# Strassen's seven products in an up projection, and a down projection with tokens on partitions

## The chip, the cores and the metric

One core of one Trainium2 chip. The metric is the device time of one execution in microseconds; the kernel before has a median of 2528.21 us over three runs (2526.31 to 2530.2).

## What is computed

One layer of a hybrid decoder trunk on 1040 tokens (16 learned meta tokens and 1024 others) of width 1024, in float32. Only the last part is touched in earnest:

```python
mixed = jax.nn.sigmoid(g_attn) * y_attn + jax.nn.sigmoid(g_ssd) * y_ssd      # y_ssd = y @ w_o_ssd, y: 2048 wide
h = layer_norm(DEEPNORM_ALPHA * h + mixed @ w_out[i], ln1_g[i], ln1_b[i])
u = causal_dwconv(h @ w_up, conv_w, conv_b)                                  # 1024 -> 2 x 2816, width 3 in time
gate, val = jnp.split(u, 2, axis=-1)
ffn = (jax.nn.silu(gate) * val) @ w_down                                     # 2816 -> 1024
h = layer_norm(DEEPNORM_ALPHA * h + ffn, ln2_g[i], ln2_b[i])
return h[:, N_META:]
```

`h` is the embedding after its own LayerNorm. Ahead of this come the input projections, latent attention in eight heads and a state-space mixer (SSD) in four groups; they stay as they are.

## The kernel before

Features lie on partitions (blocks of 128) and tokens on the free axis, in three chunks of about 348 tokens with a few tokens of overlap for the convolutions. A product is done at float32 accuracy by three passes: each operand is split into a rounded high half (ACT, L152 and L174) and the remainder (DVE, L153 and L175), and `mm3` (L158, matmuls at L163 to L165) adds high x high, low x high and high x low in PSUM. `load_w` (L138) fetches a weight block through two `wraw` buffers on the SP queue and splits it at a raised priority.

The instructions stand in the program in the order of the code; the scheduler of the framework orders each engine's queue by priority (place in the program, `load_w` ahead of its place by 400 in this part) and by when its model thinks operands and buffers are there. A tile of a pool opened over the memory of a closed one waits for the tiles that lay there. PSUM has eight banks, shared out by `cut_psum` (L109).

In the part touched:

- `transposed` (L297) stores h to HBM by chunk, and the section that starts at L635 (attention output, attention gate) reads it back and splits it. The tail of the SSD section computes gates (`gs_gate`, L745) from these tiles; four of the eight gates come after the last SSD group.
- Mixer outputs and LN1 (L899 to L981), a chunk at a time: `load_y` (L906) loads 16 tiles of y and 4 of factors and splits them; 8 output blocks with w_o_ssd (16 x 3 matmuls each), merged with the gates; 8 with w_out (8 x 3 matmuls), h added; `ln1_begin` (L921) takes the mean by a product with ones (L924), subtracts it, sums squares; `inv_root` (L177) sums over partitions (L184), takes the root on 128-partition columns (L198) and broadcasts it (L193). Weights are loaded anew in each chunk.
- FFN (L983 to L1101): `FF_PARTS` (L85) cuts the 22 blocks of the hidden width into five parts of four and one of two. `up` (L995) makes one block of the up projection for a chunk (24 matmuls), the convolution (ACT L1002, DVE L1005 twice) and Silu (L1008); `glu` (L1011) multiplies and splits. After each part the down projection adds its share to 24 SBUF accumulators (L1044 to L1047). `FHEAD` (L89) sets the first block's work on chunks 0 and 1 ahead of chunk 2, whose LN1 is still running. The last two blocks go with tokens on partitions (`last_down`, L1053, matmuls L1073 to L1075), with the accumulators added by products with ident (L1077), and LN2 follows on rows (L1081 to L1095).

## Time and profile before

| | |
|---|---|
| median of three runs | 2528.21 us |
| profiled execution | 2525.36 us |
| its span, first to last instruction | 2523.6 us |
| mean granted clock | 0.995 |
| busy: PE, DVE, ACT, GpSimd (POOL) | 2466.9, 1627.5, 1064.8, 8.5 us |
| matmuls recorded | 16023 |

PE is TensorE's matmul engine, PEld its weight loads, DVE the vector engine, ACT the scalar engine, SP the queue that issues nearly all DMAs. A busy share is the union of an engine's records; a matmul's record is longer than its share of the stream, since matmuls are pipelined, so prices are read from start times of matmuls that follow each other. PEclk is the granted clock as a share of 2.4 GHz.

### The profile page before, as it was taken

The numbers are of one execution on the slowest core, as the hardware profiler recorded it, in microseconds if no ns is written. First come the engines' busy times: TensorE is split into PE (matmuls) and PEld (weight loads), VectorE is DVE, ScalarE is ACT, GpSimd is POOL, SyncE is SP. The second block draws the span as 40 slices with busy tenths as digits, with TensorE's granted clock in tenths as the row PEclk, the third lists the DMA queues.
The fourth block names the chain that finished last, engine by engine and source line by source line (L and its number), as shares of the span: only waits on it lengthen the run. The fifth ranks groups of instructions, "written<-read, shape, count | busy, mean of one in ns | idle before, by whom it ended". The sixth has DMA issues, their size and how long they took to land.

```text
span 2523.6 us, 41608 instructions
## 1 busy us (share of the span) xinstructions
PE 2466.9 (98%) x16023; PEld 2376.7 (94%) x16023; DVE 1627.5 (64%) x4071; ACT 1064.8 (42%) x2420; POOL 8.5 (0%) x62
## 2 busy tenths in 40 slices
PE   6999999999999999999999999999999999999997
PEld 6999899899999999999999999999999999999997
DVE  6467677683356877777777568777565454554567
ACT  6345455562245554555454335444313131323331
POOL 0000000000000000000000000000000000000000
PEclk9999999999999999999999999999999999999999
DMA  5121011142222212122221566754111111111122
GB/s 201 46 65 44 27 38 44 38 138 78 67 103 91 84 62 95 66 79 82 68 89 53 168 203 209 223 167 147 36 58 39 55 42 51 47 47 51 43 86 82
DMA packets 96221, 215.22 MB, mean 85 GB/s; under 512 B 11542, under 2 KB 57366, under 8 KB 93974
## 3 DMA queue, kind: packets, MB, share of 16 engines
q1 hardware_dynamic: 95734, 211.51, 26.1%
q8 instruction: 126, 2.06, 0.3%
q0 software_dynamic: 288, 1.05, 0.1%
q14 instruction: 73, 0.60, 0.1%
HBM read 179.06 MB, written 31.35 MB: 83 GB/s over the span
## 4 chain that ended last, share of the span: by engine, by line
PE 86%; DVE 6%; DMA 4%; issue 1%; ACT 1%; SPq 0%; DVEq 0%; ACTq 0%
PE g L165 23%; PE g L163 23%; PE g L164 23%; PE c L577 3%; DMA yl<-y_d 2%; PE c L830 2%; PE c L854 1%; PE c L571 1%; PE c L834 1%; DMA wraw<-wos 1%; DVE wl L153 1%; PE c L524 1%; PE c L526 1%; PE c L528 1%; PE c L527 1%
## 5 line engine op out<-in xcount | busy, mean ns | idle before, releaser
L163 PE MATMUL g<-h,wh 128*128 128x348 f32 (+5 forms) x2616 | 845.3, 323 | 5.7 <-ACT lat L359 4.7
L165 PE MATMUL g<-h,wh 128*128 128x348 f32 (+5 forms) x2616 | 846.3, 324 | 1.2 <-DVE h L978 1.0
L164 PE MATMUL g<-h,wl 128*128 128x348 f32 (+5 forms) x2616 | 844.8, 323 | 0.0
L152 ACT CAST wh<-wraw 128x512 fp32r<-128x512 f32 (+2 forms) x474 | 287.3, 611 | 561.5 <-PE g L165 473.2
L163 PEld LDWEIGHTS g<-h,wh 128*128 128x128 f32 x2616 | 492.9, 188 | 9.6 <-ACT lat L359 5.0
L165 PEld LDWEIGHTS g<-h,wh 128*128 128x128 f32 x2616 | 492.6, 188 | 5.3 <-DVE h L978 2.9
L164 PEld LDWEIGHTS g<-h,wl 128*128 128x128 f32 x2616 | 493.4, 189 | 2.5 <-issue 2.3
L153 DVE TENSOR_TENSOR wl<-wraw,wh 128x512 fp32r<-128x512 f32 (+2 forms) x474 | 320.5, 678 | 234.8 <-ACT wh L152 229.0
L163 PE MATMUL g<-a,wh 128*128 128x348 f32 (+3 forms) x936 | 301.7, 322 | 1.6 <-DVE kn L175 1.1
L165 PE MATMUL g<-a,wh 128*128 128x348 f32 (+3 forms) x936 | 300.3, 321 | 0.0
L164 PE MATMUL g<-a,wl 128*128 128x348 f32 (+3 forms) x936 | 299.9, 320 | 0.0
L1005 DVE SCALAR_TENSOR_TENSOR u<-g,V,u 128x332 f32<-128x332 f32 (+2 forms) x264 | 150.8, 572 | 127.1 <-ACT u L1002 123.1
L163 PEld LDWEIGHTS g<-a,wh 128*128 128x128 f32 x936 | 176.2, 188 | 2.3 <-DVE kn L175 1.4
L165 PEld LDWEIGHTS g<-a,wh 128*128 128x128 f32 x936 | 176.0, 188 | 0.6 <-DVE a L175 0.5
L164 PEld LDWEIGHTS g<-a,wl 128*128 128x128 f32 x936 | 176.2, 188 | 0.0
L735 DVE SCALAR_TENSOR_TENSOR xc<-g,V,xc 128x347 f32<-128x347 f32 (+2 forms) x180 | 103.7, 576 | 41.6 <-ACT xc L731 38.8
L163 PE MATMUL g<-yh,wh 128*128 128x334 f32 (+2 forms) x384 | 122.8, 320 | 1.8 <-ACT wh L152 1.8
L165 PE MATMUL g<-yh,wh 128*128 128x334 f32 (+2 forms) x384 | 123.3, 321 | 0.0
L164 PE MATMUL g<-yh,wl 128*128 128x334 f32 (+2 forms) x384 | 122.6, 319 | 0.3 <-DVE wl L153 0.3
L1002 ACT ACTIVATE u<-g,V 128x332 f32<-128x332 f32 (+2 forms) x132 | 83.5, 633 | 78.3 <-PE g L165 76.6
L1047 DVE TENSOR_TENSOR a<-a,g 128x332 f32<-128x332 f32 (+2 forms) x96 | 49.0, 510 | 96.0 <-PE g L165 96.0
L820 ACT ACTIVATE G<-ac,tok 116x116 f32<-116x116 f32 x288 | 91.6, 379 | 42.4 <-PE c L830 42.4
(241 smaller groups left out, 3631.5 us busy)
## 6 DMA issues: line engine op xcount, KB each, us to landing
wraw<-win SPq DMA_DIRECT2D x65, 512.0 KB, 3.3
wraw<-wup SPq DMA_DIRECT2D x54, 512.0 KB, 3.3
wraw<-wos SPq DMA_DIRECT2D x48, 512.0 KB, 4.3
ac<-cs_d SPq DMA_DIRECT2D x16, 1044.0 KB, 5.7
wraw<-wout SPq DMA_DIRECT2D x24, 512.0 KB, 3.4
wraw<-wdn SPq DMA_DIRECT2D x40, 256.0 KB, 2.7
xt<-x SPq DMA_DIRECT2D x9, 512.0 KB, 5.2
wraw<-wqb SPq DMA_DIRECT2D x12, 384.0 KB, 3.7
```

The lines of the kernel that those rows point to most:

```text
L152: nc.scalar.copy(h[:, :n * ncol], r)
L153: nc.vector.tensor_sub(l[:, :n * ncol], r, f32(h[:, :n * ncol]))
L163: nc.tensor.matmul(ps, ah, bh, start=(k == 0), stop=False)
L164: nc.tensor.matmul(ps, al, bh, start=False, stop=False)
L165: nc.tensor.matmul(ps, ah, bl, start=False, stop=(k == n - 1))
L577: nc.tensor.matmul(ops[:, o0:n], vt[j][:w, hh * P:(hh + 1) * P], ptt[:w, o0:n], start=(j == 0), stop=(j == nbmax - 1))
L735: nc.vector.scalar_tensor_tensor(t[:, l:n], ps[:, hal + l - s:hal + n - s], vec("cw", (3 - s) * 24 + ct), t[:, l:n], ALU.mult, ALU.add)
L820: nc.scalar.activation(G_[:, k * S:(k + 1) * S], ac[:S, hh, C0[b] + k * S:C0[b] + (k + 1) * S], AF.Relu, bias=tok[:, 3 * b + k, 32 + hd:33 ...
L830: nc.tensor.matmul(yd[64 * hh:64 * hh + 64, k * S:(k + 1) * S], xd[:, k, hh], G[hh][:, k * S:(k + 1) * S], start=True, stop=True)
L1002: nc.scalar.activation(t[:, :n], ps[:, 2:n + 2], AF.Identity, bias=vec("fb", ti), scale=vec("fw", 2 * 44 + ti))
L1005: nc.vector.scalar_tensor_tensor(t[:, :n], ps[:, 2 - s:n + 2 - s], vec("fw", (2 - s) * 44 + ti), t[:, :n], ALU.mult, ALU.add)
L1047: nc.vector.tensor_add(A[:, :n], A[:, :n], ps[:, :n])
```

## The change

- Mixer outputs and LN1 go by two halves of 514 tokens (two of overlap) in place of three chunks; a product over 514 tokens is two matmuls of 258 and 256 columns into a pair of PSUM banks (`mm3h`).
- LN1 needs no mean: w_out is centred over its output features as it is loaded (GpSimd subtracts `wm`, the row means of w_out, for which all of w_out is loaded again as `wor` and summed), and h is centred where it is read back (`h_centered`), and kept in HBM as `hc_d`.
- Up projection by Strassen's scheme in its form with seven products: the weights of block f and f + 22 (gate and value) are cut in halves of the input width, and the tokens into two halves. Of the eight products of quarter blocks seven are left, on sums of weight quarters (GpSimd, then split) and on sums of token halves (`T1` to `T4`, formed once after LN1). The products of the first token half need LN1 of that half alone; for three blocks (`NHEAD`) these are put ahead.
- The gated products go to HBM (`gv_d`). The down projection then has tokens on partitions throughout: stationary operand 128 tokens of a hidden block, moving operand 512 columns of w_down, all 22 blocks summed in PSUM, two rounds of four token tiles; the residual enters PSUM as transposes of h1 (read back from HBM). LN2 on rows as before.
- Pools and PSUM pairs are laid out anew, some from the right end of SBUF.

The diff's core:

```diff
+HB = (NEED, NEED + 512)
+HN = 514
+HC = ((0, 258), (258, 514))
+NHEAD = 3
+KBLK = ((0, 4), (4, 8), (8, 12), (12, 17), (17, 22))
...
+            if center is not None:
+                r3 = raw[:, :kt * ncol].rearrange("p (k n) -> p k n", n=ncol)
+                nc.gpsimd.tensor_tensor(r3, r3, center.broadcast_to([P, kt, ncol]), ALU.subtract)
...
+    def mm3h(ps, lhs, rhs, start=True):
...
+            for i, (a, b) in enumerate(((ah, bh), (al, bh), (ah, bl))):
+                for c0, c1 in HC:
+                    nc.tensor.matmul(ps[:, PO + c0:PO + c1], a, b[:, c0:c1], start=(start and k == 0 and i == 0),
...
+        for c in range(3):
+            h_back(c)
+            h_centered(c)
...
+    cut_psum(0, 3)
+    pf1 = eF.enter_context(pool("F1", 16))
+    p = eD.enter_context(pool("Dr", 1, "right"))
+    pm = eM.enter_context(pool("Dm", 17, "right"))
+    pyh = eW.enter_context(pool("Dy", 33, "right"))
...
+    for k in range(KT):
+        raw = wp.tile([P, KT * P], F32, name="wraw", tag="wraw", bufs=2)
+        nc.sync.dma_start(raw, wor[k])
+        nc.vector.reduce_sum(wm[:, k], raw, axis=AX.X)
...
+    for hi in range(2):
...
+            W = load_w(wout[m], KT, center=wm)
...
+        if hi == 1:
+            eM.close()
+            pf2 = eF.enter_context(pool("F2", 40))
+            pz = eD.enter_context(pool("Dz", 8, "right"))
+        rd = inv_root(ssq, HN, 1.0 / D, LN_EPS)
...
+            for j in range(hB):
+                b11, b21 = ftile(pz, F32), ftile(pz, F32)
+                nc.sync.dma_start(b11, h1_d[j][:, HB[0]:HB[0] + HN])
+                nc.sync.dma_start(b21, h1_d[j + hB][:, HB[0]:HB[0] + HN])
+                b12, b22 = normed(j), normed(j + hB)
+                nc.vector.tensor_sub(b11, b12, b11)
+                x = dtmp("t2", "yl" if j < 3 else "ml", 3)
+                nc.vector.tensor_sub(x, b22, b11)
+                T2[j] = form(pf2, x)
+                nc.gpsimd.tensor_sub(b21, b21, x)
...
+    cut_psum(0, 4)
+    eD.close()
+    pe = eF.enter_context(pool("E1", 1))
+    rhs = {1: B1[:hB], 2: B1[hB:], 3: B2, 4: T4, 5: T1, 6: T2, 7: T3}
...
+            nc.gpsimd.tensor_sub(s3, a11, a21)
+            w[7] = wsplit(pe, s3, 5)
+            nc.gpsimd.tensor_add(s1, a21, a22)
+            nc.gpsimd.tensor_sub(s2, s1, a11)
+            w[6] = wsplit(pe, s2, 5)
+            w[5] = wsplit(pe, s1, 5)
+            nc.gpsimd.tensor_sub(s2, a12, s2)
+            w[3] = wsplit(pe, s2, 5)
+            w[4] = wsplit(pe, a22, 5)
...
+            x0 = q["x0"]
+            prod(x2, 7, w)
+            prod(x0, 6, w, False)
+            u2, u4 = etile("u2", 2), etile("u4", 2)
+            nc.scalar.copy(u2, half(x0))
+            x1 = dpair()
+            prod(x1, 2, w)
+            c11 = q["p1"]
+            nc.vector.tensor_add(c11, c11, half(x1))
+            ga = conv_up(c11, f, "ga", NHEAD)
+            prod(x0, 5, w, False)
+            nc.scalar.copy(u4, half(x0))
+        nc.vector.tensor_add(u4, u4, half(x2))
+        vb = conv_up(u4, f + NFF, "va", 2)
+        if f + 1 < NFF:
+            first(f + 1)
+        prod(x0, 3, w, False)
...
+        prod(x2, 4, w, False)
+        nc.vector.tensor_mul(gb, gb, vb)
+        nc.sync.dma_start(gv_d[f][:, 512:], gb)
+        nc.vector.tensor_add(u2, u2, half(x2))
+        va = conv_up(u2, f + NFF, "va", 2)
+        nc.vector.tensor_mul(ga, ga, va)
+        nc.sync.dma_start(gv_d[f][:, :512], ga)
...
+        for r in range(2):
+            hr = load_r(r)
...
+                        for j in range(KT):
+                            nc.tensor.matmul(pss[j // 4][:, (j % 4) * P:(j % 4) * P + P], hr[j][:, o], ident,
+                                             start=(j % 4 == 0), stop=False, is_transpose=True)
...
+                                nc.tensor.matmul(pss[q], a, b, start=False, stop=(k == NFF - 1 and i == 2))
```

## Rows read from the trace of the kernel before

**Rows 1.** The page: busy time by engine, and PE in 40 slices.
```profile
PE 2466.9 (98%) x16023; PEld 2376.7 (94%) x16023; DVE 1627.5 (64%) x4071; ACT 1064.8 (42%) x2420; POOL 8.5 (0%) x62
...
PE   6999999999999999999999999999999999999997
```
**Rows 2.** Stretches: length, busy time of each engine, PEclk, DMA share, GB/s.
```profile
545.00:740.00 195.00, 194.52 (x1244) 193.51 (x1243) 85.81 (x165) 65.79 (x147) 0.41 (x4) 1.00 0.30 97
1437.00:1660.00 223.00, 212.38 (x1315) 208.27 (x1314) 167.80 (x338) 101.84 (x192) 0.00 (x0) 0.98 0.65 204
1660.00:1765.00 105.00, 102.89 (x635) 99.51 (x634) 76.22 (x151) 49.74 (x88) 1.19 (x2) 1.00 0.50 165
1765.00:2422.00 657.00, 657.00 (x4177) 657.00 (x4176) 336.86 (x605) 192.90 (x346) 0.00 (x0) 1.00 0.15 47
2422.00:2513.20 91.20, 86.23 (x619) 83.83 (x617) 72.02 (x184) 25.08 (x50) 0.00 (x0) 0.98 0.25 84
2513.20:2523.60 10.40, 0.05 (x1) 0.00 (x0) 7.04 (x24) 0.00 (x0) 0.00 (x0) 0.71 0.38 135
```
**Rows 3.** Timeline of PE: start, duration; first and last of two unbroken runs.
```profile
172.57 0.28 PE L163 MATMUL g<-wh,a 128*116 128x256 f32 x1
...
178.83 0.28 PE L165 MATMUL g<-wl,a 128*112 128x256 f32 x1
...
2459.15 0.32 PE L163 MATMUL g<-h,wh 128*128 128x350 f32 x1
...
2461.88 0.32 PE L165 MATMUL g<-h,wh 128*128 128x350 f32 x1
```
**Rows 4.** Line 1077: count and durations of the additions by ident.
```profile
L1077 PE MATMUL c<-K,a x144: 270/274/422, 2441.3 to 2513.0; 128*128 128x128 f32 x96, 128*76 128x128 f32 x16, 128*92 128x128 f32 x16, 128*88 128x128 f32 x16
```
**Rows 5.** Timeline of PE after the last gap but one.
```profile
2499.37 0.82 PE L1073 MATMUL c<-h,a 128*88 128x256 f32 x5 [3.35 <-ACT a L174]
...
2501.38 0.41 PE L1075 MATMUL c<-h,a 128*88 128x256 f32 x1
...
2502.02 0.41 PE L1075 MATMUL c<-h,a 128*88 128x256 f32 x1
```
**Rows 6.** The chain that ended last: start, length, what.
```profile
195.86 0.89 PE c L571 x9
...
1433.51 6.00 DMA yl<-y_d
...
1536.90 0.80 PE c L924 x2
...
1740.86 0.80 PE c L184 x6
1746.45 1.46 DVE r L975 x3
```
**Rows 7.** The stretch of the last gates, columns as in rows 2.
```profile
1404.00:1440.00 36.00, 36.00 (x233) 36.00 (x232) 16.35 (x32) 11.35 (x26) 0.00 (x0) 1.00 0.66 198
```
**Rows 8.** Waits of PE: us in total, times, longest.
```profile
PE g L163 <- ACT mx L954: 4.2, 2, 2.9
...
PE g L163 <- ACT wh L152: 1.8, 1, 1.8
```
**Rows 9.** DVE and ACT by line and form: busy us, mean ns, idle before.
```profile
L153 DVE TENSOR_TENSOR wl<-wraw,wh 128x512 fp32r<-128x512 f32 x296 | 203.5, 690 | 126.2 <-ACT wh L152 122.8
...
L1093 DVE SCALAR_TENSOR_TENSOR yt<-c,mv,g 128x512 f32<-128x512 f32 x8 | 5.8, 747 | 3.7 <-DMA out<-yt 3.7
...
L152 ACT CAST wh<-wraw 128x512 fp32r<-128x512 f32 x296 | 181.7, 620 | 433.8 <-PE g L165 355.5 <-DMA wraw<-wos 41.9 <-issue 14.6
L1002 ACT ACTIVATE u<-g,V 128x348 f32<-128x348 f32 x44 | 28.2, 640 | 47.4 <-PE g L165 47.4
```
**Rows 10.** GpSimd by line and form.
```profile
L741 POOL MEMSET xc<- 128x4 f32 x20 | 2.0, 101 | 776.8 <-DVE y L867 453.4 <-PE c L780 170.8 <-DVE ga L655 152.6
L553 POOL MEMSET p<- 111x112 f32 x8 | 1.6, 195 | 0.0
```
**Rows 11.** DMA issues: count, KB each, median us to landing.
```profile
wraw<-wup SPq DMA_DIRECT2D x54, 512.0 KB, 3.3
```

More of the change, by code (lines that the diff above doesn't have):

```diff
@@ L88 @@
 WPRIO = (35, 400)
-FHEAD = 1
 LATB = 7
@@ L100, in tile_hybrid @@
 def tile_hybrid(ctx: ExitStack, tc: tile.TileContext, x, vecs, consts, cos, sin, win, wqb, wk, wv,
-                woa, wos, wout, wup, wdn, wdl, ln2, out):
+                woa, wos, wout, wor, wup, wdl, ln2, out):
     nc = tc.nc
@@ L171, in ctile, with dpair, half @@
         return psum["c"].tile([P, 512], F32, name="c", tag="c")
+    def dpair():
+        return psum["d"].tile([P, 1024], F32, name="d", tag="d")
+    def mm3h(ps, lhs, rhs, start=True):
+        n = len(lhs)
+        for k in range(n):
+            (ah, al), (bh, bl) = lhs[k], rhs[k]
+            for i, (a, b) in enumerate(((ah, bh), (al, bh), (ah, bl))):
+                for c0, c1 in HC:
+                    nc.tensor.matmul(ps[:, PO + c0:PO + c1], a, b[:, c0:c1], start=(start and k == 0 and i == 0),
+                                     stop=(k == n - 1 and i == 2), skip_group_check=not start)
+    def half(ps):
+        return ps[:, PO:PO + HN]
     def split(H, L, src):
@@ L180, in inv_root @@
         ps = ctile()
-        starts = [min(j * P, n - P) for j in range(-(-n // P))]
+        groups = [(0, n)] if n <= 512 else HC
+        starts = [a + min(j * P, b - a - P) for a, b in groups for j in range(-(-(b - a) // P))]
         k = len(starts)
@@ L195, in inv_root @@
             done = e
-        return res[:, :n]
+        return res
     def rsqrt_cols(r, v, t):
@@ L702, in tile_hybrid, with h_centered @@
                 h[k][c] = (H, L)
+                hfs[k] = of
+        def h_centered(c):
+            n = C1[c] - lo(c)
+            off = lo(c) - E0[c]
+            sm_ = p3.tile([P, 352], F32, name="hs", tag="hf", bufs=9)
+            for k in range(1, KT):
+                nc.vector.tensor_add(sm_[:, :n], (hfs[0] if k == 1 else sm_)[:, off if k == 1 else 0:][:, :n],
+                                     hfs[k][:, off:off + n])
+            ps = ctile()
+            nc.tensor.matmul(ps[:, :n], ones, sm_[:, :n], start=True, stop=True)
+            nc.scalar.activation(sm_[:, :n], ps[:, :n], AF.Copy, scale=1.0 / D)
+            for k in range(KT):
+                nc.vector.tensor_sub(hfs[k][:, off:off + n], hfs[k][:, off:off + n], sm_[:, :n])
+                nc.sync.dma_start(hc_d[k][:, lo(c):C1[c]], hfs[k][:, off:off + n])
+        for c in range(3):
+            h_back(c)
+            h_centered(c)
         for m in range(3):
@@ new lines, in prod, with etile, conv_up @@
+    def prod(ps, q, w, start=True):
+        mm3h(ps, w[q], rhs[q], start)
+    def etile(name, bufs, n=HN):
+        return pe.tile([P, n], F32, name=name, tag=name, bufs=bufs)
+    def conv_up(src, ti, tag, bufs):
+        t = etile(tag, bufs, 512)
+        nc.scalar.activation(t, src[:, 2:], AF.Identity, bias=vec("fb", ti), scale=vec("fw", 2 * 44 + ti))
+        for k in (1, 2):
+            nc.vector.scalar_tensor_tensor(t, src[:, 2 - k:HN - k], vec("fw", (2 - k) * 44 + ti), t, ALU.mult, ALU.add)
+        if ti < NFF:
+            nc.scalar.activation(t, t, AF.Silu)
+        return t
@@ new lines, in tile_hybrid, with first @@
+    st = [dict() for _ in range(NFF)]
+    def first(f):
+        q = st[f]
+        if f < NHEAD:
+            q["w"] = wrest(f, None)
+            return
+        q["w"] = wrest(f, {})
+        q["x0"] = dpair()
+        prod(q["x0"], 1, q["w"])
+        q["p1"] = etile("p1", NHEAD)
+        nc.scalar.copy(q["p1"], half(q["x0"]))
+    tops = {}
+    for f in range(NHEAD):
+        tops[f] = wtop(f)
+        q = st[f]
+        q["x0"] = dpair()
+        prod(q["x0"], 1, tops[f])
+        q["p1"] = etile("p1", NHEAD)
+        nc.scalar.copy(q["p1"], half(q["x0"]))
+        for g in ([f - 1] if f else []) + ([f] if f == NHEAD - 1 else []):
+            x = st[g].pop("x0")
+            prod(x, 2, tops[g], False)
+            st[g]["ga"] = conv_up(half(x), g, "ga", NHEAD)
@@ new lines, in load_g, with load_r @@
+        def load_g(r, k):
+            with tc.high_priority(wprio[0]):
+                t = p.tile([P, 512], F32, name="gv", tag="gv", bufs=3)
+                nc.sync.dma_start(t, gv_d[k][:, 512 * r:512 * r + 512])
+                H = ph.tile([P, 512], F32R, name="dh", tag="dh")
+                L = ph.tile([P, 512], F32R, name="dl", tag="dl")
+                split(H, L, t)
+            return H, L
+        def load_r(r):
+            res = []
+            with tc.high_priority(wprio[0]):
+                for k in range(KT):
+                    t = p.tile([P, 512], F32, name="hr", tag="hr", bufs=8)
+                    nc.sync.dma_start(t, h1_d[k][:, OUT0 + 512 * r:OUT0 + 512 * r + 512])
+                    nc.scalar.activation(t, t, AF.Copy, scale=ALPHA)
+                    res.append(t)
+            return res
@@ L1141, in _prepare @@
     wup = full(inp["w_up"][0], 2 * NFF, KT)
-    wdn = full(inp["w_down"][0], KT, NFF)
-    wdl = np.stack([inp["w_down"][0][f * P:(f + 1) * P] for f in range(*FF_PARTS[-1])])
+    wor = inp["w_out"][0].reshape(KT, P, D)
+    wdl = inp["w_down"][0].reshape(NFF, P, D)
     vecs = np.zeros((P, NVC), np.float32)
```

412 lines of the change are left out of this document (207 added, 205 removed).

## The prediction

> **What bounds the kernel now.** I read the page first: TensorE (PE) is busy 2466.9 us of a span of 2523.6, and no slice of the span but the first and the last is below nine tenths [rows 1]. So the columns streamed through PE set the time. The profiled execution took 2525.4 us; the median of the three runs, 2528.2, is 0.11% more, and I add that at the end. 0.2% (5 us) is about what a measurement of this kernel can tell from no change.
>
> Then the stretches from the first mixer output (1437 us) on, which hold all that is edited but a small piece [rows 2]. PE is idle there for 10.6 us (to 1660), 2.1 (to 1765), 0 (657 us of up and down projection without a gap), 5.0, and for the last 10.4 us, in which only the last LayerNorm and the store run: 28 us. Where the clock column is below 1, matmuls ran partly at 1.2 GHz: 0.02 x 223 + 0.02 x 91 = 6 us more. So 34 us of this part are not column time.
>
> Then the start times of matmuls in a row [rows 3], since durations overlap. 256 columns: 172.57 to 178.83 us over 53 steps, 118.1 ns. 350 columns: 2459.15 to 2461.88 over 17 steps, 160.6 ns. That is 0.461 and 0.459 ns a column: no fixed price of a matmul can be seen, and each has a weight load of its own. So halving a matmul is free down to 256 columns. 512 columns don't occur; in proportion they take 235 ns, by the line through 256 and 350 columns 232.
>
> **The sum, PE.** Up projection before: 44 blocks x 8 x 3 matmuls at 334, 346 and 350 columns, 1056 x 1030 x 0.46 ns = 500 us. After: 22 blocks x 7 products x 4 x 3 matmuls over 514 columns, each cut into 258 and 256 (237 ns): 1848 x 0.237 = 438 us. **-62.** Matmuls rise from 3168 to 3696, columns fall by an eighth.
>
> Down projection before: 20 blocks x 8 x 3 over 1024 columns, 480 x 1024 x 0.46 = 226 us; the last two blocks 216 x 0.118 = 25.5; their additions of the residual by ident, 144 records [rows 4] at the 0.099 us of a transpose (nine in 0.89 us [rows 6]), 14. After: 1056 x 0.235 = 248, and 64 transposes of h1, 6. **-11.**
>
> Mixer outputs before 576 x 1034 x 0.46 = 274 us, after 1152 x 0.237 = 273. The three ones products for the mean (0.8 us each [rows 6]) go, and the column sums and broadcasts of inv_root drop from 18 to 10 each: **-4** together. PE in all: **-77.**
>
> **The sum, waits.** The 34 us above all belong to seams that are rebuilt, so I take them out and price the new seams.
>
> (a) Start of the mixer outputs. Before, the y tiles of a third come in while the last gates run, at 198 GB/s [rows 7], with DMA waits for y in the chain of up to 6 us [rows 6]. Now the y of half of the tokens must be there for the first output, 20 tiles of 263 KB, and wm needs all of wor (8 x 524 KB) ahead of them in program order, on the same SP queue and the same two wraw buffers: 3.4 MB become 9.5 MB, 30 us more at that rate. That overlaps with output m = 0 (11.4 us) and with what slack the gates leave. I take 14; bounds 2 (the wait there before, 1.8 [rows 8]) and 28. For the second half the y tiles load under w_out (46 us): 3.
>
> (b) The last output of a half goes through DVE, DVE, ACT, DVE before w_out can use it; before, these waits were 4.2 us, two of them [rows 8]. 3; bounds 0 and 6.
>
> (c) LN1 of the second half up to the first Strassen product that needs it. After the last w_out product: residual, square, sum (2.4 us); column sums to normalised rows (1740.86 to 1746.45, 5.6 us [rows 6]); then on DVE 8 normalisations, 8 differences and 20 low halves, 36 x 0.69 to 0.75 us [rows 9] = 26 us. That makes 34 us, of which T2 and T3 (products 6 and 7) are ready after some 25. PE has the six head products of B1, 6 x 2.85 = 17 us. The weights of products 7 to 4 lie in E1, opened where Dz and Dr were; I assume that some wait for the last form (no row shows placement). 17; bounds 8 and 25. In the kernel before FHEAD covered this seam to 2.1 us with two whole chunks of tokens.
>
> (d) Within the up projection PE takes 7 x 2.85 = 19.9 us a block. DVE: 7 low halves x 0.69, 8 convolution steps and 3 sums x 0.75, 2 products x 0.69 = 14.5 us; ACT 7 x 0.62 + 9 x 0.7 = 10.6 [rows 9]. Covered in the mean; a PSUM pair must be read between two products into it, which another product (2.85 us) covers except in the first three blocks. 5; bounds 0 and 25. The products' stores and loads add 0.5 MB a block to a queue that moves 47 GB/s in this stretch [rows 2]: nothing.
>
> GpSimd takes the weight sums, four of 512 columns a block, and 1024 columns for each w_out block. No row has such an operation; the nearest is a fill of 112 columns in 195 ns against 101 ns for four columns [rows 10], so 0.5 us at least for 512, and at most perhaps three times DVE's 0.69, 2 us. I take 1.1, nearer to the fill, beside other work.
>
> (e) Up to down. hr lands where p1, ga and the last operands lay: conversion of the last block (some 6 us), a DMA (3.3 us for 512 KB [rows 11]), the scale, then the transposes that open the accumulation. 12; bounds 6 and 18.
>
> (f) The end: last LayerNorm and store, 10.4 us before [rows 2]; the piece is of the same size: 9, bounds 8 and 11.
>
> (g) The clock. After the gap of 3.35 us PE ran 256 columns in 213 ns instead of 118 (2501.38 to 2502.02, three steps [rows 5]), which is the 1.2 GHz level, for some 3 us: 1.7 us for each of the three long gaps, 5.
>
> (h) Centring h when it is read back: 45 DVE operations of about 0.52 us in a stretch where DVE is busy 86 of 195 us [rows 2], three PE products of 0.8, 24 stores: 1; bounds 0 and 6.
>
> New seams: 14 + 3 + 3 + 17 + 5 + 12 + 9 + 5 + 1 = 69. Sum: 2525.4 - 77 - 34 + 69 = 2483, and with 0.11% **2486 us**.
>
> **Two rules weighed.** The matmul price carries everything: 0.46 ns a column at 256 and at 350 columns [rows 3]. The Trainium skill (TensorE: Matmul & The Clock Gate, Back-to-back issue gap) gives a stream of load and matmul about 81 ns at 128 and 131 ns at 512 columns, mostly a fixed price; an estimate between these is 98 ns at 257 and 109 at 343, by which the up projection would go from 345 to 362 us, a loss where I count a gain of 62. The rows of this trace contradict it.
>
> DVE's 690 ns for a difference of 512 columns [rows 9] were measured with GpSimd idle, which was busy 8.5 us in all [rows 1]. The Trainium skill (SBUF - State Buffer, Who interferes with whom) says that a DVE instruction with two SBUF inputs and a GpSimd one that reads SBUF exclude each other for a whole instruction. No run here shows that yet.
>
> **The rivals.**
> 1. The seams stay as cheap as before: wor loaded under the gates, weights of E1 not held. For it: only 2.1 us at the LN1 seam before. Against it: the bytes of (a) and DVE's 26 us of (c). 2525.4 - 77 = 2448, with 0.11% 2451.
> 2. Late DVE: if its 14.5 us and GpSimd's 4 x 1.1 can't overlap, they make 18.9 of 19.9 us, and queues in order then hold a PSUM pair now and then, 1.5 us a block: +33, 2519.
> 3. **Slower: GpSimd sets the pace.** If DVE has to wait out each sum of t us, a block takes 14.5 + 4t once that passes 19.9. The change loses when a block is 2.2 us longer than PE needs, t = 1.9; at t = 2.5 it is 22 x 4.6 = 101 us, 2587. For it: no row bounds t firmly. Against it: 2 us is three times DVE's own.
> 4. Pairs of halves cost more than the runs of 256 columns do. Up projection and mixer outputs have 6000 of them, so the change loses from 126 ns a piece instead of 118.5; at 130 ns +69, 2555. For it: no row has pairs on one weight tile in two PSUM banks. Against it: 53 even steps [rows 3].
> That seven products were not seven eighths of the columns is excluded by the code: 22 x 7 x 12 x 514 against 44 x 24 x 1030.
>
> **Chances.** Forecast 0.57, rival 1 0.20, rival 2 0.15, rival 3 0.05, rival 4 0.03. Within the forecast (a), (c), (d) and (e) may each be off by about 10, together some 20: 2466 to 2506. The range takes in rival 1 and most of rival 2: 2446 to 2518. Faster by over 0.2% means below 2523: the first three cases but for a tail of rival 2, 0.90; within 0.2% 0.03; slower 0.07.
>
> **What would show it.** Right: in the up stretch starts 0.118 us apart, 19.9 us a block, PE full; 512-column matmuls 0.235 us apart; gaps at the start of the mixer outputs (released by DMA of y), at LN1 (by forms of T2, T3 or by wl) and at the first transposes (by hr), with a granted clock below 1 after each. Wrong: starts further apart than 0.12 us at full clock (rival 4); PE waiting on ACT or DVE in every block with DVE over 90% busy, its 512-column differences well above 0.69 us (rivals 2 and 3); no gap over 5 us at the seams (rival 1).

## The result, and the profile after

The changed kernel takes **2679.49 us** (median of four runs, 2674.55 to 2684.01) against 2529.2 for the kernel before beside it: a ratio of **1.0595** [1.0573, 1.0617]. The forecast was 2486 with a range up to 2518, so it is missed by 193 us and on the wrong side.

The page answers to [rows 1]: PE's busy time is the same (2463.5 us against 2466.9) in a span of 2672.8, so it is idle for 209 us instead of 57. The slices below nine tenths begin where the mixer outputs begin, and those of the clock stand with them; the mean granted clock is 0.956 (0.995 before).

```profile
PE 2463.5 (92%) x16451; PEld 2322.7 (87%) x16451; DVE 1646.7 (62%) x3819; ACT 1111.7 (42%) x2434; POOL 174.8 (7%) x174
...
PE   6999999999999999999996897978888878879998
...
PEclk9999999999999999999998997988989888889999
```

By stretches (columns as in [rows 2]): h read back and attention output; mixer outputs and w_out of the first half, then of the second; LN1 to the first products that need it; the up projection; the seam to the down projection; the first part of that.

```profile
545.00:740.00 195.00, 189.00 (x1178) 186.09 (x1177) 98.91 (x198) 57.45 (x126) 0.29 (x3) 0.98 0.36 117
...
1440.00:1620.00 180.00, 150.77 (x1208) 149.42 (x1206) 93.90 (x128) 52.19 (x86) 15.50 (x8) 0.92 0.51 167
1620.00:1760.00 140.00, 124.06 (x961) 121.91 (x962) 84.36 (x130) 49.91 (x84) 11.39 (x6) 0.90 0.50 163
1760.00:1830.00 70.00, 47.91 (x353) 47.17 (x352) 49.48 (x74) 29.94 (x51) 22.92 (x14) 0.80 0.36 121
1830.00:2380.00 550.00, 466.11 (x3482) 460.98 (x3481) 306.21 (x426) 200.41 (x328) 116.52 (x85) 0.89 0.20 62
2380.00:2420.00 40.00, 23.76 (x144) 20.36 (x143) 20.81 (x31) 20.86 (x35) 1.23 (x2) 0.79 0.66 229
2420.00:2540.00 120.00, 120.00 (x532) 97.48 (x531) 63.84 (x120) 47.72 (x85) 0.00 (x0) 1.00 0.56 189
```

No long stretch is full but the down projection. In 550 us of up projection PE is idle for 84 and the clock is 0.89; before, [rows 2] had 657 us without a gap at a clock of 1.00. No other engine is the bound there: DVE is busy 56%, ACT 36%, GpSimd 21%. So PE waits for something that is late, not for something that is full. PE's waits name it (us in total, times, longest):

```profile
PE d L191 <- ACT u L1191: 75.5, 19, 5.0
PE d L191 <- ACT wh L160: 26.9, 1, 26.9
...
PE c L1285 <- ACT hr L1251: 15.4, 3, 7.9
PE d L191 <- ACT r L1028: 14.4, 1, 14.4
PE d L191 <- ACT f L198: 13.1, 5, 10.2
```

Nineteen times, once in each block that has no products put ahead, a product waits for the copy `u4` (L1191), which empties a PSUM pair between two products into it. PE's order there is Strassen's products 3 and 4 of one block, 7, 6, 2 and 5 of the next, and 1 of the block after that; `u4` takes product 5 out of the pair before product 3 of the same block goes into it, and product 1 is its cover. The other four rows are the seams: the start of the mixer outputs, the transposes of the down projection, LN1 to up projection, and the second half's y.

**One block in the timeline** shows why the copy is late. L1086 loads weights into one of two landing buffers, L1109 to L1115 are the sums on GpSimd, L198 and L199 a cast and a low half, L1191 is the copy; rows of PE are L191.

```profile
2016.21 0.80 PE L191 MATMUL d<-f,wh 128*128 128x258 f32 x2 [3.98 <-ACT u L1191]
...
2024.93 0.62 ACT L198 CAST wh<-wraw 128x512 fp32r<-128x512 f32 x1 [1.81 <-issue]
...
2025.59 0.69 DVE L199 TENSOR_TENSOR wl<-wraw,wh 128x512 fp32r<-128x512 f32 x1
...
2026.31 0.33 SPq L1086 DMA_DIRECT2D wraw<-wup  x1
...
2030.17 1.28 POOL L1109 TENSOR_TENSOR s<-wraw 128x512 f32<-128x512 f32 x1 [20.13 <-DMA wraw<-wup]
...
2031.40 1.30 POOL L1111 TENSOR_TENSOR s<-wraw 128x512 f32<-128x512 f32 x1
...
2032.14 1.11 DVE L199 TENSOR_TENSOR wl<-s,wh 128x512 fp32r<-128x512 f32 x1 [3.04 <-ACT wh L198]
2032.78 1.62 POOL L1112 TENSOR_TENSOR s<-s,wraw 128x512 f32<-128x512 f32 x1
...
2035.86 1.30 POOL L1115 TENSOR_TENSOR s<-wraw,s 128x512 f32<-128x512 f32 x1 [1.46 <-DVE wl L199]
...
2037.18 15.08 SPq L1086 DMA_DIRECT2D wraw<-wup  x2
...
2040.48 0.62 ACT L198 CAST wh<-wraw 128x512 fp32r<-128x512 f32 x1 [3.25 <-DMA wraw<-wup]
...
2042.58 0.56 ACT L1191 COPY u<-d 128x514 f32<-128x514 f32 x1
...
2043.19 0.80 PE L191 MATMUL d<-f,wh 128*128 128x258 f32 x2 [3.88 <-ACT u L1191]
```

Read it backwards from 2043.19. The copy ran at 2042.58. It stood in ACT's queue behind a cast of fresh weights (2040.48), for which ACT had been idle for 3.25 us, and behind two more casts and a Silu; the fresh weights are for a later block, and nothing on PE was waiting for them. They came late because their load could be issued only at 2037.18, when GpSimd's last sum (L1115) had read the buffer's old content. That sum came after the three sums ahead of it, and the first of these waited for the other landing buffer (load issued at 2026.31). That buffer was freed by the low half at 2025.59, whose cast (2024.93) takes a weight tile that Strassen's product 4 gives up; the profile names no releaser for this cast, but by the code the tile is that one, and PE finished product 4 at about 2024.9. So there is a **loop through the two landing buffers**: from the end of product 4 to the restart of PE it takes 2043.2 - 2024.9 = 18.3 us. PE has five products to do in that time, 5 x 2.89 = 14.4 us; the difference, 3.9 us, is the gap. After the gap that ends at 2016.21 PE runs at the 1.2 GHz level for some 6 us (six matmuls in 1.29 us from 2016.80, in 0.72 from 2022.76), 2.9 us lost. Together 20.2 + 3.9 + 2.9 = 27.0 us a block, 2016.21 to 2043.19, where 19.9 was forecast.

The clock's part differs from block to block: after the gaps PE worked for 2.8 to 5.9 us at the lower level. This is the stretch of 17 blocks, from one restart of PE to another (columns as in [rows 2]):

```profile
1909.32:2367.25 457.93, 384.96 (x2857) 381.05 (x2857) 242.35 (x340) 163.87 (x271) 92.69 (x68) 0.88 0.19 59
```

A block takes 26.9 us on average: PE is idle for 4.3 of them, and its 2857 matmuls, 344 us at the full-clock spacing of 0.1204, took 385.0, so that 2.4 us a block are lost at the lower level.

### The profile page after: what moved, and what is told of

It is laid out like the page before. It is cut to its first block, busy times and chain, and to the rows that moved or that the text cites. A ratio compares the mean times of both kernels' runs of the same rounds, so it can differ in the third digit from the quotient of the medians.

```text
span 2672.8 us, 42479 instructions
## 1 busy us (share of the span) xinstructions
PE 2463.5 (92%) x16451; PEld 2322.7 (87%) x16451; DVE 1646.7 (62%) x3819; ACT 1111.7 (42%) x2434; POOL 174.8 (7%) x174
## 4 chain that ended last, share of the span: by engine, by line
PE 74%; DMA 8%; DVE 6%; POOL 3%; issue 3%; ACT 3%; SPq 0%; DVEq 0%; POOLq 0%; ACTq 0%
PE d L191 15%; PE g L171 11%; PE g L173 11%; PE g L172 11%; PE c L1294 9%; DMA wraw<-wup 5%; PE c L605 3%; PE c L881 2%; ACT wh L198 2%; PE c L905 1%; PE c L599 1%; POOL s L1112 1%; DVE wl L199 1%; PE c L885 1%; POOL s L1111 1%
## 5 line engine op out<-in xcount | busy, mean ns | idle before, releaser
L191 PE MATMUL d<-f,wh 128*128 128x258 f32 (+1 forms) x4000 | 693.4, 296 | 142.6 <-ACT u L1191 75.5
L191 PEld LDWEIGHTS d<-f,wh 128*128 128x128 f32 x4000 | 591.6, 203 | 151.2 <-ACT u L1191 79.5
L171 PE MATMUL g<-h,wh 128*128 128x348 f32 (+3 forms) x1560 | 507.2, 325 | 8.8 <-ACT h L198 4.8
L172 PE MATMUL g<-h,wl 128*128 128x348 f32 (+3 forms) x1560 | 507.5, 325 | 0.0
L173 PE MATMUL g<-h,wh 128*128 128x348 f32 (+3 forms) x1560 | 507.0, 325 | 0.0
L191 PE MATMUL d<-f,wl 128*128 128x258 f32 (+1 forms) x2000 | 423.0, 294 | 0.0
L191 PEld LDWEIGHTS d<-f,wl 128*128 128x128 f32 x2000 | 331.1, 202 | 0.4 <-DVE wl L161 0.2
L171 PEld LDWEIGHTS g<-h,wh 128*128 128x128 f32 x1560 | 294.9, 189 | 12.4 <-ACT h L198 5.2
L172 PEld LDWEIGHTS g<-h,wl 128*128 128x128 f32 x1560 | 295.0, 189 | 2.4 <-issue 2.4
L173 PEld LDWEIGHTS g<-h,wh 128*128 128x128 f32 x1560 | 294.5, 189 | 2.8 <-issue 2.4
L199 DVE TENSOR_TENSOR wl<-wraw,wh 128x512 fp32r<-128x512 f32 x154 | 102.3, 689 | 161.3 <-ACT wh L198 127.6
L198 ACT CAST wh<-wraw 128x512 fp32r<-128x512 f32 x154 | 90.8, 617 | 239.7 <-PE c L1294 100.3
L199 DVE TENSOR_TENSOR wl<-s,wh 128x512 fp32r<-128x512 f32 x88 | 72.8, 828 | 157.5 <-ACT wh L198 157.2
L171 PE MATMUL g<-a,wh 128*128 128x348 f32 (+2 forms) x456 | 148.8, 326 | 1.5 <-DVE kn L199 1.1
L173 PE MATMUL g<-a,wh 128*128 128x348 f32 (+2 forms) x456 | 148.2, 325 | 0.0
L172 PE MATMUL g<-a,wl 128*128 128x348 f32 (+2 forms) x456 | 147.7, 324 | 0.0
L198 ACT CAST wh<-s 128x512 fp32r<-128x512 f32 x88 | 54.1, 619 | 214.6 <-POOL s L1109 101.2
```

The source lines that it names most:

```text
L171: nc.tensor.matmul(ps, ah, bh, start=(k == 0), stop=False)
L172: nc.tensor.matmul(ps, al, bh, start=False, stop=False)
L173: nc.tensor.matmul(ps, ah, bl, start=False, stop=(k == n - 1))
L191: nc.tensor.matmul(ps[:, PO + c0:PO + c1], a, b[:, c0:c1], start=(start and k == 0 and i == 0), stop=(k == n - 1 and i == 2), skip_group_c ...
L198: nc.scalar.copy(H, src)
L199: nc.vector.tensor_sub(L, src, f32(H))
```

## The experiments

Medians, ratios to the kernel before run beside each, and what each came to against the changed kernel (2679.5). The last column compares different sessions, in which the kernel before took between 2528.3 and 2531.8 us, so that differences of some 3 us in it mean nothing:

| run | edit | us | ratio, 95% | |
|---|---|---|---|---|
| e1 | third landing buffer | 2590.4 | 1.0239 [1.0215, 1.0264] | -89 |
| e2 | copy ahead of the casts | 2584.2 | 1.0217 [1.0194, 1.0240] | -95 |
| e6 | weight sums on DVE | 2569.6 | 1.0164 [1.0140, 1.0187] | -110 |
| e3 | eight plain products | 2597.0 | 1.0271 [1.0246, 1.0295] | -83 |
| e7 | LN1's PSUM pair, down seam | 2671.9 | 1.0569 [1.0552, 1.0586] | -8 |
| e8 | start of both mixer halves | 2652.6 | 1.0484 [1.0467, 1.0500] | -27 |
| e9 | e2, e6, e7, e8 together | 2520.0 | 0.9967 [0.9954, 0.9980] | -160 |
| e10 | e3 with e7, e8 | 2560.5 | 1.0122 [1.0108, 1.0137] | -119 |
| e11 | e9, six products ahead of the forming | 2508.4 | 0.9916 [0.9902, 0.9929] | -171 |
| e12 | e11, weight sums on GpSimd | 2547.8 | 1.0071 [1.0057, 1.0085] | -132 |
| e13 | e11, LN1's sums on DVE | 2507.9 | 0.9912 [0.9899, 0.9926] | -172 |
| e14 | e13, first block's weights early | 2504.8 | 0.9907 [0.9890, 0.9924] | -175 |

### The loop: e1, e2, e6

The theory is the loop; the rivals are that GpSimd and DVE set the pace (rival 3 of the prediction), and that a PSUM pair between two products has too little cover.

**e1.**

```diff
-        raw = wp.tile([P, KT * P], F32, name="wraw", tag="wraw", bufs=2)
+        if ti < NFF:
+            raw = wp.tile([P, KT * P], F32, name="wraw", tag="wraw", bufs=2)
+        else:
+            raw = pe.tile([P, KT * P], F32, name="wrb", tag="wrb", bufs=1)
```

> The raw weights of the value half (a21, a22) get a landing buffer of their own, so the two shared ones serve the gate half alone. Theory (the loop): a block of the up projection takes 27.0 us because the second load of a block lands only when GpSimd's last sum has freed its buffer, and ScalarE, in order, holds the copy u4 behind a cast that waits for that landing. With the third buffer the next load is under way a block earlier: a block 20.2 to 21.5 us (168 matmuls x 0.1203 us = 20.2), the wait of d (line 191) on the copy u (line 1191) falls from 75 us to under 15, the time to 2555-2580. Rival A (GpSimd's sums of 1.3-1.6 us and VectorE exclude each other and set the pace): buffers change nothing, 2665-2685. Rival B (a pair of sum tiles is read between two products into it and the cover is simply too short): the gap of about 4 us stays, 2665-2685.

**e2.**

```diff
-                w.update({1: wsplit(wp, a11, 4), 2: wsplit(wp, a12, 4)})
+                with tc.issue_after(cps[f - 2]) if f - 2 in cps else ExitStack():
+                    w.update({1: wsplit(wp, a11, 4), 2: wsplit(wp, a12, 4)})
...
-            nc.scalar.copy(u4, half(x0))
+            cps[f] = nc.scalar.copy(u4, half(x0)).ins
```

> The two landing buffers stay; only ScalarE's order changes: the casts of the first two operands of block g stand behind the copy u4 of block g-2 and no longer ahead of it. The loop: the copy no longer waits for a landing, so the product after it starts at once: a block 20.2 to 22.5 us, time 2555-2600; if the landing itself (buffer free 2037.2, landed 2040.5) then makes the operands of the next product late, the wait moves to casts (h, line 198) and a block stays at 24-27 us, 2620-2680. Rivals A and B: no change, 2665-2685.

**e6.**

```diff
-            nc.gpsimd.tensor_sub(s3, a11, a21)
+            nc.vector.tensor_sub(s3, a11, a21)
...
-            nc.gpsimd.tensor_add(s1, a21, a22)
-            nc.gpsimd.tensor_sub(s2, s1, a11)
+            nc.vector.tensor_add(s1, a21, a22)
+            nc.vector.tensor_sub(s2, s1, a11)
...
-            nc.gpsimd.tensor_sub(s2, a12, s2)
+            nc.vector.tensor_sub(s2, a12, s2)
```

> The four sums of weights of each block move from GpSimd (1.28-1.62 us each) to VectorE. Rival A (GpSimd sets the pace, by its own length or by exclusion): a block falls to about 20.5 us, 2550-2570. The loop: it stays a loop, only its chain is shorter by 4 x 0.6-0.9 us less the queueing on VectorE, so a block of 24 to 27 us, 2620-2680.

**Measured.** Each of the three takes 89 to 110 us away. PE's waits for the copy and the stretch from 2000 to 2200 us of e1, then e2, then e6:

```profile
PE d L191 <- ACT u L1194: 26.3, 19, 4.1
...
2000.00:2200.00 200.00, 187.38 (x1532) 185.32 (x1532) 133.73 (x183) 88.65 (x147) 49.03 (x36) 1.00 0.23 72
```

```profile
PE d L191 <- ACT u L1193: 18.7, 18, 3.8
...
2000.00:2200.00 200.00, 191.66 (x1568) 189.61 (x1567) 129.74 (x185) 88.03 (x146) 51.84 (x39) 1.00 0.25 77
```

```profile
PE d L191 <- ACT u L1191: 15.7, 16, 2.3
...
2000.00:2200.00 200.00, 192.48 (x1575) 190.43 (x1574) 154.07 (x226) 89.68 (x147) 0.00 (x0) 1.00 0.24 77
```

A block has 168 matmuls, so a block takes 200 x 168 / 1532 = 21.9 us in e1, 21.4 in e2 and 21.3 in e6, and the clock in this stretch is 1.00. e2 changes an order and nothing else: no operation is shorter, none leaves its engine, and GpSimd's sums are as long as before. So the order in ACT's queue is a cause by itself, and rivals A and B, which expected no change from e1 and e2, fall in the form in which they were put.

e2 came out as the loop expected. e1 fell short of it: 2590.4 for 2555 to 2580, a block of 21.9 us for 20.2 to 21.5, and 26.3 us of waits for under 15. Its timeline shows what is left, a gap of some 1.2 us a block:

```profile
2017.41 1.41 DVE L199 TENSOR_TENSOR wl<-wraw,wh 128x512 fp32r<-128x512 f32 x1
...
2020.30 0.63 ACT L1136 ACTIVATE ga<-ga 128x512 f32<-128x512 f32 x1 [1.44 <-DVE ga L1134]
```

The loads are in time now, but the copy (2020.84) still stands in ACT's queue behind the Silu of the gate branch, for which ACT waited 1.44 us. Silu waits for the convolution on DVE, and ahead of that is a low half that took 1.41 us instead of 0.69 beside GpSimd's last sum (2016.98 to 2018.27). In e2 the same Silu is ahead of the copy, after a wait of 1.10 us.

But e6 landed on rival A's number (2550 to 2570), not on mine (2620 to 2680). My expectation took the shorter chain off the block, and that was too little: what counts is the gap, 18.3 - 14.4 us. Four sums at 0.69 in place of 1.28, 1.29, 1.62 and 1.30 us (groups below) shorten the chain by 2.7 us, the gaps between 2000 and 2200 us fall to 0.5 to 0.9 us (one is 2.0), and with them goes the time lost at the 1.2 GHz level. So GpSimd does not set the pace as a busy engine; its slow sums are a link of the loop. GpSimd's groups of the changed kernel between 1900 and 2200 us (busy us, mean ns, idle before):

```profile
L1112 POOL TENSOR_TENSOR s<-s,wraw 128x512 f32<-128x512 f32 x12 | 19.4, 1618 | 0.9
L1115 POOL TENSOR_TENSOR s<-wraw,s 128x512 f32<-128x512 f32 x12 | 15.5, 1295 | 17.5 <-DVE wl L199 17.5
L1111 POOL TENSOR_TENSOR s<-wraw 128x512 f32<-128x512 f32 x11 | 14.2, 1291 | 0.0
L1109 POOL TENSOR_TENSOR s<-wraw 128x512 f32<-128x512 f32 x11 | 14.2, 1289 | 218.7 <-DMA wraw<-wup 218.7
```

GpSimd was idle for 218.7 of these 300 us waiting for weights to land.

### Strassen itself: e3

Eight plain products, no sums of weights or tokens; weight loads and PSUM use are those of a plain product (the edit replaces the product section by this loop).

```diff
+        for ti in (f, f + NFF):
+            W = load_w(wup[ti], KT)
+            for hi, B in halves:
+                ps = dpair()
+                mm3h(ps, W, B)
+                gv[f, ti, hi] = conv_up(half(ps), ti, "gt%d" % hi, 4)
```

> Everything else of the change stays, but the up projection is made of eight plain products of halves and no sums: per block 192 matmuls in place of 168, and one weight load per tile. Theory: the products then run back to back, 192 x 0.1203 = 23.1 us a block against 27.0 now, 22 blocks: -86 us; and the gap of 14.4 us ahead of the projection shrinks since only the plain operand is formed: -5 to -14. Time 2575-2595. If instead the price of matmul pairs or the clock were at fault, eight products would cost an eighth more than seven: 2679 + 74 = 2750.

```profile
2000.00:2200.00 200.00, 200.00 (x1659) 200.00 (x1659) 87.94 (x122) 57.16 (x87) 0.00 (x0) 1.00 0.20 67
```

2597.0, 2 us above the expected range. With a seventh more matmuls in the up projection the kernel is 83 us faster, since PE is full; the spacing is 200 / 1659 = 0.1206 us. So neither the matmul pairs nor the clock by itself is at fault, and seven products cost more than eight as they were fed here.

### The seams: e7, e8

**e7.** The broadcast root of LN1 is copied out of its PSUM pair, and the residual tiles `hr` get a pool that opens first over the up projection's operands (its second set of loads moved to a later place).

```diff
-        rd = inv_root(ssq, HN, 1.0 / D, LN_EPS)
+        nc.scalar.copy(ssq, inv_root(ssq, HN, 1.0 / D, LN_EPS))
+        rd = ssq
...
-    with pool("Eh", 25) as ph, pool("Ew", 1) as p:
+    with pool("Er", 8) as pr, pool("Ew", 1) as p, pool("Eh", 25) as ph:
```

> Two seams alone, the up projection's blocks as they are. (1) LN1's broadcast factor is copied from its PSUM pair to SBUF at once. Theory: the first product of the up projection waits 14.4 us for that pair, which eight scalings read one after the other; with the copy the wait falls to 2-6 us. Rival: it waits for operands that LN1 forms, and stays at 12-15. (2) The residual tiles of the down projection get the memory that the first operands of the up projection leave, not the last. Theory: their loads start a block earlier and the 15.4 us before the first transposes fall to 0-5; rival: it is the bytes of weights and products loaded beside them (229 GB/s), and 10-15 stay. Time 2650-2662 by the theories, 2675-2685 by the rivals.

```profile
PE d L191 <- ACT p L1159: 21.2, 1, 21.2
...
PE c L1289 <- DVE u L1206: 3.9, 1, 3.9
```

2671.9, between the two, and by the ratios (1.0569 and 1.0595, their intervals overlap) not clear of the changed kernel's time; the waits tell more. (2) held: the 15.4 us before the transposes became a 3.9 us wait for a DVE sum of the last block. (1) **moved**: the wait for the pair is gone, three products run, and the fourth then waits 21.2 us for the copy `p1` of the first, which stands in ACT's queue behind all the casts of LN1's operands. It is the same kind of fault as in the blocks.

**e8.**

```diff
-                nc.sync.dma_start(ts_d[m][:, lo(c):C1[c]], t[:, :n])
+                nc.scalar.dma_start(ts_d[m][:, lo(c):C1[c]], t[:, :n])
...
-    with pool("G", 3, "right") as pgs, pool("C", 1) as p:
+    with pool("G", 3) as pgs, pool("C", 1) as p:
...
-                sq = dtmp("sq", "yl", 3)
+                sq = dtmp("sq", "sq", 2)
```

and the loop over `wor` (the column means) stands ahead of the last gates.

> The start of the mixer and the start of its second half alone: the gate stores go out on ScalarE's queue, the gate tiles lie where the first y tiles don't come to lie, the column means of the output weights are read before the last gates, and the squares of LN1 get buffers of their own. Theory: y loads wait in SP's order behind gate stores and for their memory, then 16 tiles x (scaling + cast + low half) run ahead of the products; with the edits they run beside the gates: the wait of 26.9 us falls to 0-8, that between the halves (10.2 in one piece) to 0-3, time 2640-2655. Rival: VectorE's two operations a tile (16 x 1.4 us = 22 us) set the start whenever the loads come, 20 us stay, and 2665-2680.

```profile
1461.80 0.70 PE L191 MATMUL d<-f,wh 128*128 128x258 f32 x2 [2.08 <-ACT f L198]
1467.71 0.51 PE L191 MATMUL d<-f,wh 128*128 128x258 f32 x2 [1.97 <-ACT f L198]
```

2652.6, as expected: these two are what is left of the gap of 26.9 us at the start, and the longest wait for the second half's y falls from 10.2 to 0.8 us. DVE's work on y did not set the start; the four edits were not tried apart. Some 10 us come back as longer waits for DVE in two roots (L218: 9.6 us in place of 2.5, and 8.0 in place of 4.9), probably since the sums over `wor` and the second half's y now stand on DVE there; for the first of the two e11 bears it out.

### Everything: e9, and plain with the seams: e10

> Everything together: sums on VectorE, the copy ahead of the casts on ScalarE, and the edits of both seam runs. If the parts add: 2570 (sums on VectorE alone) - 22 - 10 (mixer) - 10 (LN1) - 12 (down start) - 0 to 8 (copy order) = 2508-2520, 0.3 to 0.9% faster than before. If a seam only moves (a late operand of the next product, VectorE now 77% busy), 2530-2550.

> The eight plain products with the same seam edits, no sums: what Strassen's seven products are worth once they are not held up. By the matmuls alone plain costs 24 x 22 x 0.1203 = 63 us more, less the stalls that remain in the seven-product blocks (about 1 us x 20) and the operands that LN1 need not form (8): 30-40 us above the run with everything, 2540-2560. If it comes out at or under that run, the saved products are paid back in full by what feeds them.

```profile
PE d L191 <- ACT p L1161: 20.6, 1, 20.6
...
2000.00:2200.00 200.00, 199.10 (x1648) 198.69 (x1647) 159.02 (x235) 92.62 (x153) 0.00 (x0) 1.00 0.25 79
```

e9 is 2520.0, faster than before by 0.33%, its upper expectation, with the moved wait of LN1 still in it. The up projection is now full: 1648 matmuls in 200 us, 20.4 us a block, with DVE 80% busy. e10 is 40.6 us slower than e9 (2560.5), just above its expectation. That is the net worth of seven products here: e9's wait of 20.6 us at LN1, with 2 us lost to the clock behind it, has no counterpart in e10, so within the blocks seven products fed in time are worth some 63 us against eight, which is the 63 us of the saved matmuls.

### The start of the up projection: e11 to e14

**e11.** The loop over the first blocks' products 1 and 2 stands before `normed` is called for the second half, `p1` and `ga` have a pool of their own (`E0`), and the means of w_out are read one at a time after each gate.

```diff
-        return pe.tile([P, n], F32, name=name, tag=name, bufs=bufs)
+                return (pe0 if name in ("p1", "ga") else pe).tile([P, n], F32, name=name, tag=name, bufs=bufs)
```

> The run with everything, and two edits more: the first six products of the up projection, whose operands are the first half's alone, are put ahead of the forming of the second half's operands, with memory of their own for their results (p1, ga), so that ScalarE's copies of them no longer stand behind that forming; the column means of the output weights are read one by one beside the gates. Theory: the wait of 20.6 us for the copy p vanishes as six products (17 us) run beside the forming; what is left is the end of the forming, 0-8 us. Time 2500-2510, 0.7-1.1% below before. Rival: the forming itself (33 us from 1771 to 1804, VectorE stretched by GpSimd) lasts longer than the products cover, 10-16 us stay: 2510-2520.

**e12** is e11 with the sums of e6 undone.

> The same with the weights' sums back on GpSimd: what GpSimd's sums cost once ScalarE's order is mended. If the hold of the copy was all, a block stays at 20.2 us and the time within 5 us of the run with the sums on VectorE; if sums of 1.3-1.6 us, or the exclusion of VectorE by GpSimd, still set a part of the pace, a block is 21 to 21.6 us (as with the copy order alone) and the time 15-28 us above it.

**e13** is e11 with LN1's sums on DVE.

```diff
-                nc.gpsimd.tensor_sub(b21, b21, x)
+                nc.vector.tensor_sub(b21, b21, x)
...
-                nc.gpsimd.tensor_sub(rs[j], rs[j + hB], rs[j])
+                nc.vector.tensor_sub(rs[j], rs[j + hB], rs[j])
```

> As the run with the products put ahead, and LN1's eight sums of 514 columns moved from GpSimd to VectorE as well. They lie beside VectorE's work that the trace shows stretched from 0.69 to 1.1-1.75 us a piece. If that exclusion costs more than the moved work (8 x 0.69 = 5.5 us on VectorE), the forming ends 2-6 us earlier and the time falls by 0-6; if not, it rises by 0-5.

e11 is 2508.4, in the theory's range, but mostly by something else: the wait for `p1` is gone (20.6 us to 0.9), six products run, and the seventh waits 17.5 us, longer than the rival had it. Of the 11.6 us gained some 7 are the means of w_out, now spread (the root's wait L218 falls from 9.6 to 2.3 us). The seventh product waits not for its tokens but for its weights, in both e11 and e13; the timeline of e13, and then the first weight sum of e12:

```profile
1794.84 2.50 DVE L199 TENSOR_TENSOR f<-f 128x514 fp32r<-128x514 f32 x4
1797.37 0.69 DVE L1150 TENSOR_TENSOR s<-wraw 128x512 f32<-128x512 f32 x1
...
1800.10 1.01 PE L191 MATMUL d<-f,wh 128*128 128x258 f32 x3 [17.88 <-ACT wh L198]
```

```profile
1797.65 1.26 POOL L1150 TENSOR_TENSOR s<-wraw 128x512 f32<-128x512 f32 x1 [11.23 <-DVE f L199]
```

The first weight sum (L1150) starts as soon as the last low half of the tokens is done, while the tokens for this product were ready at 1785.7 (the low half that began at 1785.00). In e13 that alone could be DVE's queue, since DVE does the sum itself and was busy until then. e12 decides it: there GpSimd does the sum, has been idle for 11.23 us, and still waits for the same low half. So it is the tile's memory, in the pool that opens over LN1's.

e13 equals e11 (0.4 us). That doesn't say that GpSimd beside DVE costs nothing. From the root to the first weight sum (columns as in [rows 2]), e11 and then e13:

```profile
1761.07:1800.10 39.03, 22.75 (x154) 22.03 (x154) 33.39 (x44) 24.67 (x41) 12.40 (x8) 0.76 0.28 97
```

```profile
1759.14:1797.37 38.23, 22.40 (x154) 21.89 (x154) 32.67 (x52) 24.61 (x41) 0.00 (x0) 0.72 0.28 99
```

DVE does eight instructions more in e13 (5.5 us at 0.69), in no more busy time. So the lengthening beside GpSimd's eight sums had cost about as much as the moved work, and moving them gained nothing.

e12 gives the weight sums' price in a mended kernel: 39 us, more than the 15 to 28 expected.

```profile
2000.00:2200.00 200.00, 191.72 (x1567) 189.64 (x1567) 129.96 (x185) 89.73 (x149) 52.94 (x39) 1.00 0.24 72
```

A block there takes 200 x 168 / 1567 = 21.4 us, which is 22 us of it over the blocks. The seams are longer too: 19.6 us for the seventh product instead of 17.5, waits of 1.9, 3.5, 1.4 and 2.1 us in the first blocks and one of 3.7 in the last.

**e14.** The weights of Strassen's products 6 and 7 of the first block are formed ahead of LN1's operands in temporaries (`sq`) and in `wh`, `wl` of the weight pool.

```diff
+                raw0 = wload(0) + wload(NFF)
+                d6, d7 = dtmp("d6", "sq", 2)[:, :512], dtmp("d7", "sq", 2)[:, :512]
+                nc.vector.tensor_add(d6, raw0[2], raw0[3])
+                nc.vector.tensor_sub(d6, d6, raw0[0])
+                w0 = {6: wsplit(wp, d6, 4)}
+                nc.vector.tensor_sub(d7, raw0[0], raw0[2])
+                w0[7] = wsplit(wp, d7, 4)
```

> As the run with LN1's sums on VectorE, and the first block's weight sums (for its sixth and seventh products) are formed ahead of the second half's operands, in temporaries that LN1 no longer needs, and no longer in memory that opens only when all operands are formed. Theory: the wait of 17.9 us ahead of the seventh product after the start is for those weights (sums at 1797.4, the operand itself ready at 1785.7); it falls to 4-9 us, and the time to 2495-2501. Rival: the next product then waits for its own operands or weights as long, 2504-2510.

```profile
1788.82 0.51 PE L191 MATMUL d<-f,wh 128*128 128x258 f32 x2 [3.27 <-ACT f L198]
1802.94 0.79 PE L191 MATMUL d<-f,wh 128*128 128x258 f32 x2 [8.05 <-ACT wh L198]
```

2504.8, which is in the rival's range and not in the theory's: the 17.9 us became 3.3 for the tokens and then 8.1 for the next weights, which still lie in the late pool. It has the lowest time of all, 0.93% under the kernel before, but e13 is 0.88% under the one run beside it, with overlapping intervals, so the last step is seen in the waits and not shown by the times.

## Why the prediction was wrong

**The step that failed is (d)**, "a PSUM pair must be read between two products into it, which another product (2.85 us) covers except in the first three blocks", priced at 5 us with bounds 0 and 25. The cover is there: by 2.89 us a product, counted back from the gap, Strassen's product 5 ended at about 2036.4 and product 1, its cover, ran to 2039.3, and the copy takes 0.56 us. But the copy started at 2042.58. (d) costed DVE and ACT as sums of busy time (14.5 and 10.6 of 19.9 us) and did not ask what stands ahead of the copy in ACT's queue, nor how long a landing buffer is held. What (d) says of the loads, "nothing", was true of bytes (62 GB/s) and wrong of buffers: two buffers, two loads a block, and a last reader at the end of four dependent sums. Measured: 75.5 us of waits in the nineteen blocks, which (d) took for covered, instead of 5. In the first three blocks, for which it had its price, PE waited 0.9 and 1.4 us for the sums out of PSUM. e2, which moves only the casts behind the copy, shows that the order in ACT's queue is a cause; e1 and e6, that the loop's length is the other side of it.

**(g), the clock,** was priced for three gaps at 1.7 us. The gaps of the blocks cost some 42 us (2.4 a block on average, 2.9 in the one shown). The mechanism was right; the count hung on (d).

**(a)** 14 + 3 us were 26.9 and 10.2, the first near its upper bound of 28. The direction was right (9.5 MB and the wor loads ahead of them); beyond it the y loads stood in SP's queue behind the gate stores until 1450, and the second half's y shared its buffers with the squares of LN1, so that it did not load under w_out. Both are read from the trace and the code; e8 took the waits away by four edits at once. **(b)** 3 us cost nothing: PE has no wait over 0.2 us at either start of w_out.

**(c)** 17 us was about the size (14.4, then 3.0 at the next wait, 4.6 in the root), for another reason: the first product waited for the PSUM pair that holds the root, not for T2, T3 or weights. So the size was luck. The reason forecast, weights in a pool opened over Dz and Dr, stood behind it and came out in e11 and e13 at 17.5 and 17.9 us. **(e)** 12 was 15.4. **(f)** 9 was 8.7. **(h)** 1 us was 6.0, its upper bound (PE 189.0 of 195 us).

**The PE term held** but for 12 of its 77 us (below). In e9's full stretch the spacing is 0.121 us a matmul and 20.4 us a block for 19.9 forecast. **Rival 4's** worry was real but small: in the unbroken runs of e3 pairs on one weight tile are 0.1206 us apart for 0.1185, 13 us over 6000 pieces. The first weighed rule (TensorE: Matmul & The Clock Gate, Back-to-back issue gap, in the Trainium skill) stays contradicted: a matmul of 512 columns takes 0.232 us here (26 from 2469.61 to 2475.64), as the line of [rows 3] gave.

**Rival 2** had the mechanism in kind: queues in order that hold a PSUM pair. It had it on DVE, for want of time there (18.9 of 19.9 us), at 1.5 us a block; it was ACT's queue, with DVE 53% and ACT 36% busy between 1900 and 2200, and about 6.7 us a block (4.3 idle, 2.4 lost to the clock). So the sign set for it, DVE over 90% busy, did not show.

**Rival 3** named an engine that is a link of the loop, with the wrong mechanism. t was 1.29 to 1.62 us, under the 1.9 at which the rival said the change loses, and DVE was 53% busy between 1900 and 2200. Its outcome (2587) came nearer than any other, by a loop that it did not contain.

**The miss adds up**, counted on PE in the two profiled executions. Idle time: the new seams were forecast at 64 us (69 without the clock's 5) and are 182 by the stretches above: mixer halves with the first root 45.1 for 20, LN1 22.1 for 17, up projection 83.9 for 5, start of the down projection 16.2 for 12, end 8.7 for 9, (h) 6.0 for 1; that is 118 too much. Work at the 1.2 GHz level, by the records of the granted clock, cost 70 us where 7 was forecast (5, and 2 that stay from before): 63, of which 45 in the up projection. The stream itself is 65 us shorter than before and not 77: 12, which the spacing of pairs explains (13). That makes 193 of 193, where about 1 us less idle time ahead of the change and a median further above the profiled execution cancel.

**Left open:** the 11.3 us (3.3 and 8.1) at the start of the up projection that e14 still has; with buffers for the first block's remaining weights the second part may go, which was not tried.

## What to carry to other kernels

Sums of busy time bound a stage from below only; a queue in order adds every wait of what stands ahead. For each copy that frees a PSUM pair, ask what is ahead of it on its engine and what that waits for, and for each pair of landing buffers write out the loop (freed, issued, landed, read by its last reader) and set its length against the work that PE has in the same time. Where a wait is removed, look for the next operand in line before counting the gain: the 14.4 us at LN1 became 21.2 (the copy), then 17.5 (the weights), then 3.3 and 8.1.
